# Grouped issue of the small fp32 products in a two-layer hybrid decoder step

## The chip, the cores and the metric

The kernel runs on one core of one Trainium2 chip. The metric is device microseconds of one execution; the time before is the median of 3 runs. The engines of the profile are PE (matrix products, with PEld its weight loads), DVE (vector), ACT (scalar and activations), POOL and SP; times are in us.

## The reference, cut to what matters

One inference step over a prompt of 512 tokens and 8 samples of 8 tokens each. A layer is

```
h    = rmsnorm(x); proj = h @ W_in             # 1024 -> all heads' inputs
mix  = [SSD(Mamba-2) | window attention | HGRN2 | RG-LRU](proj)
x    = x + mix @ W_out
x    = x + square(relu(rmsnorm(x) @ W_up)) @ W_down
```

and there are two of them, then a last RMSNorm. The change touches two of the four mixers:

```
# window attention: 4 blocks of 128 queries, a block sees its own and the previous 128 keys
logits = q k^T * 64**-0.5 + rel_bias(masked)   # 4 heads
p      = softmax([logits, sink])[..., :-1];  o = p @ v
# the 8 samples do the same against their cached 128 keys and their own 8
# SSD: chunks of the prompt and the samples each add a state
states = einsum('bcshn,bcsh,bcshp->bchpn', B, decay_s, x * dt)
S      = S * chunk_decay + states
```

New states, keys and values are outputs beside y.

## The kernel before, in words

All 576 tokens (512 of the prompt, 64 of the samples) lie as columns, and the features on partitions. Each large projection (`product`, L329 to L348) is done in three products of a high and a low part, 128x128 weights against 288 columns at a time, and this is most of what PE does: 8712 of its products are such "projection products" (tiles `pi` input, `pd` output and part of the down projection, `p` and `pu` MLP, `pl` the last), and 928 program-level matmuls are small fp32 products of the mixers. An fp32 product of the program shows as more than one record in the trace.

The kernel is written in a framework whose scheduler puts every engine's instructions into one fixed order when the program is built. It goes by the order in which the code issues them, except that `high_priority` lifts an instruction, and it lets an instruction overtake others whose inputs or buffers it holds to be later; `issue_after(x)` forbids those in its scope to stand ahead of x on x's engine. On the chip each engine then goes through its list strictly in order and waits at an instruction whose inputs are not there. So projection products fill the places on PE where a mixer's small product is not ready yet, as far as some are left that may run.

PSUM is split into 3 banks for projections (`mmbank`) and 5 for everything else (`bank`). The output projection (`outproj`, L1015) comes in two halves: `outproj(0)` needs only HGRN2 and SSD and has 192 products in a layer; `outproj(1)` needs RG-LRU and the attention and has 192 too, of which, by the three banks, 18 can run on the RG-LRU's part before the attention's output `mixh` exists. These 384 are what can fill PE while the attention (`swa`, L892 to L1012) works.

In `swa` the samples come first: 64 scores `ls`, the softmax in the tiles `L` (exponentials L941, scales L949), eight transposes `pts` (L954) copied to `PT`, values `aos`. Then four blocks of the prompt as generators, run by `staggered` (L138): scores `lg` (L978) and their masked maximum on DVE (L982); softmax (`ng` L985, exponentials L988 on ACT, `mx` L990, `sm` on DVE to L992); then a head at a time the scale on ACT (L1000), its transposes `pt` on PE (L1002), the copy to `PT` (L1003), at last the values `ao` (L354, from `tiled`) and the cast to `mixh` (L1008). The generators run one step apart, so that a block's scores, its neighbour's softmax and the next one's transposes are issued in turn. `PT` has 3 buffers and `L` has 4; a block takes two of each.

In the SSD, `dtt` (L685) is 15 small transposes of dt and its sums; `su` (L781) is a chunk's state and `sus` (L793) the samples'; `y` (L354) is the output's group of products.

Of the kernel before, what the change touches and what calls it, by code (L numbers as in the profile page):

```python
# [2 lines left out]

# [1 line left out]

# [8 lines left out]
AF = mybir.ActivationFunctionType  # L14
# [6 lines left out]
NP_ = 512  # L21
NB, NT = 8, 8
# [10 lines left out]
SLOT = 608  # L33
# [98 lines left out]
def seqs(t, w=NT):  # L132

    o = NP_ if w == NT else NP_ + 3
    return t[:, o : o + NB * w].rearrange("p (b t) -> p b t", b=NB)


def staggered(parts):  # L138

    n = 0  # L140
    while parts:
        n += 1
        for p in parts[:n]:
            if next(p, True):
                parts.remove(p)
                n -= 1


class Kern:
# [200 lines left out]
    def tiled(self, products):  # L350


        for n, (out, w, x) in enumerate(products):
            self.nc.tensor.matmul(out, w, x, start=n < 2, stop=n >= len(products) - 2, skip_group_check=True)  # L354

    def silu(self, out, in_):
        return self.nc.scalar.activation(out, in_, AF.Silu)
# [292 lines left out]
    def ssd_dt(self):  # L650

        nc, V, S, P = self.nc, self.nc.vector, self.nc.scalar, self.ssp
        dt, t1 = (P.t("b", SLOT, bufs=2)[:4, :T] for _ in range(2))
        ac, ed = (P.t("c", 640, bufs=SC)[:4, :T] for _ in range(2))
        rs = P.t("Bt", 640)[:4, :T]
        self.dma(rs, self.I["reset"])
        for h in range(2):
            a = slice(TH * h, TH * h + TH)
            ps = self.bank("pdt")[:4, :TH]
            nc.tensor.matmul(ps, self.con("sel4"), self.dtq[:, a], start=True, stop=True)  # L660
            V.tensor_tensor(dt[:, a], ps, self.rs[:4, a], op=ALU.mult)
        V.tensor_scalar(dt, dt, self.par("dtb", 0, 4), None, op0=ALU.add)
        S.activation(t1, dt, AF.Abs)
        S.activation(t1, t1, AF.Exp, scale=-1.0)
        S.activation(t1, t1, AF.Ln, bias=self.c1[:4])
        V.scalar_tensor_tensor(dt, dt, 0.0, t1, op0=ALU.max, op1=ALU.add)
        na = self.small([4, 1], "na")
        S.activation(na, self.par("alog", 0, 4), AF.Exp)
        V.tensor_scalar(na, na, -1.0, None, op0=ALU.mult)
        V.tensor_scalar(t1, dt, na, None, op0=ALU.mult)  # L670
        V.tensor_tensor_scan(ac, rs, t1, 0.0, op0=ALU.mult, op1=ALU.add)
        for a, w in ((slice(0, NP_), 128), (slice(NP_, T), NT)):
            cv = ac[:, a].rearrange("p (n t) -> p n t", t=w)
            V.tensor_tensor(ed[:, a].rearrange("p (n t) -> p n t", t=w),
                            cv[:, :, w - 1 : w].broadcast_to(list(cv.shape)), cv, op=ALU.subtract)
        S.activation(ed, ed, AF.Exp)
        dr = self.acd = self.dp.tile([4, T], F32, name=f"acd{self.li}")
        self.q(QC).dma_start(dr, ac)

        p2 = self.bank("dtt")  # L680
        pv = p2[:, :60].rearrange("p (c w h) -> p c w h", c=5, w=3)
        for ci in range(5):
            n = 128 if ci < 4 else NS
            for w, t in enumerate((dt, ac, ed)):
                nc.tensor.transpose(pv[:n, ci, w], t[:, 128 * ci : 128 * ci + n], self.ident[:4, :4])  # L685
        self.dtt = self.small([128, 5, 3, 4], "dtt")
        S.copy(self.dtt[:, :4], pv[:, :4])
        S.copy(self.dtt[:64, 4], pv[:64, 4])

        self.cs, self.el = [], self.small([128, 2, 12], "el")  # L690
        self.acj = self.small([128, 2, NS], "acj")
        for j in range(2):
            t = P.t("cs", T, bufs=2)
            for g in range(2):
                self.q(QC).dma_start(t[64 * g : 64 * g + 64], dr[2 * g + j].partition_broadcast(64))
                self.q(QC).dma_start(self.acj[64 * j : 64 * j + 64, g], dr[2 * g + j, NP_:T].partition_broadcast(64))
            S.activation(t, t, AF.Exp)
            V.tensor_copy(self.el[:, j, :4], t[:, :NP_].rearrange("p (c t) -> p c t", c=4)[:, :, 127])
            self.cs.append(t)
        S.activation(self.acj, self.acj, AF.Exp)  # L700

    def ssd(self):
        nc, V, S, li, P = self.nc, self.nc.vector, self.nc.scalar, self.li, self.ssp
# [22 lines left out]
        Bt = P.t("Bt", 640)  # L726
# [6 lines left out]
        for ci in range(4):  # L733
            a = slice(128 * ci, 128 * ci + 128)
            for g in range(2):
                nc.tensor.matmul(G[g][:, a], B[64 * g : 64 * g + 64, a], C[64 * g : 64 * g + 64, a], start=True, stop=True)
        for g in range(2):
            rg = slice(64 * g, 64 * g + 64)
# [36 lines left out]
            V.tensor_tensor(vs(xs[:64, NP_:640]), vs(p2[:64, :128]), ws(0), op=ALU.mult)  # L775
            V.tensor_tensor(vs(xd[:64, NP_:640]), vs(xs[:64, NP_:640]), ws(2), op=ALU.mult)

            for ci in range(4):
                a = slice(128 * ci, 128 * ci + 128)
                pu = self.bank("su")  # L780
                nc.tensor.matmul(pu[rg, :128], Bt[:, 128 * ci + 64 * g : 128 * ci + 64 * g + 64], xd[:, a], start=True, stop=True)  # L781
                if ci == 0:
                    V.tensor_copy(new[ci][rg], pu[rg, :128].rearrange("p (j n) -> p j n", j=2))
                    continue
                for j in range(2):
                    V.scalar_tensor_tensor(new[ci][rg, j], new[ci - 1][rg, j], self.el[rg, j, ci : ci + 1],
                                           pu[rg, 64 * j : 64 * j + 64], op0=ALU.mult, op1=ALU.add)
            S0 = P.t("S0", [NB, 64])
            self.dma(S0, self.I["sS0"][li, :, g])
            ve = P.t("b", SLOT, bufs=2)  # L790
            self.by_sequence(ve, Bt[:64, NP_ + 64 * g : NP_ + 64 * g + 64])
            ps = self.bank("sus")
            nc.tensor.matmul(ps, xd[:64, NP_:640], ve[:64, :512], start=True, stop=True)  # L793
            V.tensor_tensor(S0, S0, self.acj[:, g].rearrange("p (b t) -> p b t", b=NB)[:, :, NT - 1 : NT].broadcast_to([128, NB, 64]), op=ALU.mult)
            V.tensor_tensor(S0, S0, ps.rearrange("p (b n) -> p b n", b=NB), op=ALU.add)
            self.dma(self.O["sssm"][li, g], S0.rearrange("p b n -> p (b n)"))
# [95 lines left out]
    def swa(self, Q, K, Vv):  # L892
# [53 lines left out]
        for i in range(2):  # L946
            for u in range(2):
                l = Ls[i][:, u, :192]
                S.activation(l, l, AF.Copy, scale=sm[:, i, u : u + 1])  # L949
        pc, pn = P.t("PT", [2, 256], bufs=3), P.t("PT", [2, 256], bufs=3)  # L950
        for dst, rows, a in ((pc, 128, slice(0, 128)), (pn, 64, slice(128, 192))):
            ps = self.bank("pts")
            for k in range(4):
                nc.tensor.transpose(ps[:rows, 128 * k : 128 * k + 128], Ls[k // 2][:, k % 2, a], self.ident)  # L954
            S.copy(dst[:rows].rearrange("p a n -> p (a n)"), ps[:rows])
        p2 = self.bank("aos")
        kv = lambda i: slice(64 * i, 64 * i + 64)
# [8 lines left out]
        sk0 = PC["sink"][0]  # L966
        sinks = self.prm[:, li, sk0 : sk0 + 4]

        def block(nb):
            s0, n = (128 * (nb - 1), 256) if nb else (0, 128)  # L970
            nk = n // 128
            a = slice(128 * nb, 128 * nb + 128)
            L = [P.t("L", [2, 256], bufs=4) for _ in range(2)]
            mx, sm, ng = (self.small([128, 4], c) for c in ("mx", "sm", "ng"))
            lg = [self.bank("lg").rearrange("p (e n) -> p e n", e=2) for i in range(2)]
            for e in range(2):
                for i in range(2):
                    nc.tensor.matmul(lg[i][:, e, :n], Q[e][kv(i), a], K[kv(i), s0 : s0 + n], start=True, stop=True)  # L978
            for i in range(2):
                for e in range(2):  # L980
                    h = 2 * i + e
                    V.tensor_tensor_reduce(out=L[i][:, e, :n], in0=lg[i][:, e, :n], in1=bias[:, h, 256 - n :], scale=1.0,  # L982
                                           scalar=sinks[:, h : h + 1], op0=ALU.add, op1=ALU.max, accum_out=mx[:, h : h + 1])
            yield
            V.tensor_scalar(ng, mx, -1.0, None, op0=ALU.mult)  # L985
            for h in range(4):
                l = L[h // 2][:, h % 2, :n]
# [2 lines left out]
            S.activation(mx, mx, AF.Exp)  # L990
            V.tensor_tensor(sm, sm, mx, op=ALU.add)
            V.reciprocal(sm, sm)  # L992
            yield
            PT = [P.t("PT", [2, 256], bufs=3) for _ in range(2)]
            for i in range(2):
                pt = self.bank("pt").rearrange("p (e n) -> p e n", e=2)
                for e in range(2):
                    h = 2 * i + e
                    l = L[i][:, e, :n]
                    S.activation(l, l, AF.Copy, scale=sm[:, h : h + 1])  # L1000
                    for k in range(nk):
                        nc.tensor.transpose(pt[:, e, 128 * k : 128 * k + 128], l[:, 128 * k : 128 * k + 128], self.ident)  # L1002
                S.copy(PT[i][:, :, :n], pt[:, :, :n])  # L1003
            po = self.bank("ao").rearrange("p (e n) -> p e n", e=2)[:, :, :128]
            at = lambda i, k: s0 + 128 * k + 64 * i
            self.tiled([(po[kv(i), e], vt[:, at(i, k) : at(i, k) + 64], PT[i][:, e, 128 * k : 128 * k + 128])
                        for k in range(nk) for e in range(2) for i in range(2)])
            S.copy(oh[:, :, a], po)  # L1008
            V.tensor_tensor(ol[:, :, a], po, oh.bitcast(F32)[:, :, a], op=ALU.subtract)

        staggered([block(nb) for nb in range(4)])
        return oh, ol  # L1012


# [380 lines left out]
```

## Time and profile before

| | |
|---|---|
| median of 3 runs | 1359.47 us (1356.86 to 1362.58) |
| profiled execution | 1355.2 us, its span 1353.4 us |
| TensorE granted clock, mean | 0.998 of full |
| PE busy | 1328.0 us, 98% |
| DVE busy | 1028.5 us, 76% |
| ACT busy | 658.2 us, 49% |
| DMA, mean | 97 GB/s |

PE is busy in every fortieth of the span but the first, where it starts at 7 us. The other engines have room on the average. A row of a timeline gives start, duration, engine, line, operation, the tile written from the tiles read, the size, and in brackets the idle time ahead of it with what ended that; consecutive rows of one kind are merged with a count.

### The profile page before, as it was taken

The page shows a single profiled execution, that of the slowest core. Times are in us where ns is not written, and L with a number is a line of the kernel's source. Part 1 is how long each engine was busy: PE and PEld are TensorE (multiplying, and loading weights), DVE is VectorE, ACT ScalarE, POOL GpSimd, SP SyncE. Part 2 cuts the span into 40 slices and gives each one's busy share as a digit, 9 for nine tenths or more (in the row PEclk, how much of TensorE's full clock was granted, in tenths as well). Part 3 has the DMA queues.
Part 4 walks back from the last instruction along what each step waited for, and adds up shares of the span by engine and source line. Part 5 has one row for each costly group of instructions (what it writes and reads, how often), then busy time and mean ns, then how long its engine had stood idle before and what let it go on. Part 6 is the DMA issues. An engine that isn't in the chain of part 4 may idle for free.

```text
span 1353.4 us, 25452 instructions
## 1 busy us (share of the span) xinstructions
PE 1328.0 (98%) x10384; PEld 1279.6 (95%) x10384; DVE 1028.5 (76%) x2043; ACT 658.2 (49%) x1175; POOL 63.3 (5%) x126
## 2 busy tenths in 40 slices
PE   7999999999999999999999999999999999999997
PEld 7999899799999999999999998988999999999997
DVE  7788888488678677776669678886977677777755
ACT  6565436766243334333354774477653243334325
POOL 2201102000000000000000001100000000000000
PEclk9999999999999999999999999999999999999999
DMA  6324414123213222322331233231223213222312
GB/s 237 104 87 139 165 68 144 48 79 110 77 65 110 78 92 81 113 75 86 131 121 47 98 117 128 94 111 48 79 81 123 78 63 109 79 82 91 115 58 71
DMA packets 39831, 131.36 MB, mean 97 GB/s; under 512 B 6089, under 2 KB 8241, under 8 KB 39681
## 3 DMA queue, kind: packets, MB, share of 16 engines
q1 hardware_dynamic: 29312, 102.12, 21.9%
q0 software_dynamic: 6512, 22.64, 5.0%
q10 hardware_dynamic: 3888, 4.97, 1.2%
q8 instruction: 82, 1.34, 0.4%
q14 instruction: 37, 0.30, 0.1%
HBM read 120.32 MB, written 11.34 MB: 97 GB/s over the span
## 4 chain that ended last, share of the span: by engine, by line
PE 86%; DVE 7%; ACT 3%; issue 2%; DMA 0%; SPq 0%; DVEq 0%; ACTq 0%
PE pd L339 33%; PE p L1102 21%; PE pi L339 15%; PE pu L339 6%; PE pl L1255 2%; PE sc L554 2%; DVE lo L326 1%; DVE a L444 1%; PE ss L402 1%; PE ao L354 1%; ACT hi L326 1%; DVE A L562 1%; DVE qE L550 1%; PE y L354 1%; PE lg L978 1%
## 5 line engine op out<-in xcount | busy, mean ns | idle before, releaser
L326 ACT CAST hi<-raw 128x1024 fp32r<-128x1024 f32 x134 | 140.2, 1046 | 297.1 <-PE pd L339 144.6
L339 PE MATMUL pd<-fh,hi 128*128 128x288 f32 x960 | 284.1, 296 | 0.0
L339 PE MATMUL pd<-fl,hi 128*128 128x288 f32 x960 | 284.0, 296 | 0.0
L339 PE MATMUL pd<-fh,lo 128*128 128x288 f32 x960 | 282.8, 295 | 0.0
L339 PE MATMUL pi<-xh,hi 128*128 128x288 f32 x704 | 210.6, 300 | 7.6 <-ACT xh L377 7.1
L339 PE MATMUL pi<-xl,hi 128*128 128x288 f32 x704 | 210.4, 300 | 1.1 <-DVE xl L378 1.1
L339 PE MATMUL pi<-xh,lo 128*128 128x288 f32 x704 | 211.1, 300 | 0.0
L326 DVE TENSOR_TENSOR lo<-raw,hi 128x1024 fp32r<-128x1024 f32 x134 | 163.6, 1222 | 27.3 <-ACT hi L326 26.7
L1037 DVE TENSOR_TENSOR x<-x,pd 128x288 f32<-128x288 f32 x240 | 108.2, 451 | 97.9 <-PE pd L339 97.8
L339 PEld LDWEIGHTS pd<-fh,lo 128*128 128x128 f32 x960 | 180.9, 188 | 0.0
L339 PEld LDWEIGHTS pd<-fh,hi 128*128 128x128 f32 x960 | 180.4, 188 | 0.0
L339 PEld LDWEIGHTS pd<-fl,hi 128*128 128x128 f32 x960 | 180.4, 188 | 0.0
L339 PEld LDWEIGHTS pi<-xh,hi 128*128 128x128 f32 x704 | 133.0, 189 | 10.1 <-ACT xh L377 7.1
L339 PEld LDWEIGHTS pi<-xh,lo 128*128 128x128 f32 x704 | 132.9, 189 | 6.0 <-issue 5.2
L339 PEld LDWEIGHTS pi<-xl,hi 128*128 128x128 f32 x704 | 132.9, 189 | 3.6 <-DVE xl L378 1.7
L1102 PE MATMUL p<-Th,ul 128*128 128x288 f32 x312 | 92.2, 296 | 0.0
L1102 PE MATMUL p<-Tl,uh 128*128 128x288 f32 x312 | 92.1, 295 | 0.0
L1102 PE MATMUL p<-Th,uh 128*128 128x288 f32 x312 | 92.0, 295 | 0.0
L1102 PE MATMUL p<-xl,uh 128*128 128x288 f32 x312 | 91.9, 295 | 0.0
L1102 PE MATMUL p<-xh,ul 128*128 128x288 f32 x312 | 91.9, 295 | 0.0
L1102 PE MATMUL p<-xh,uh 128*128 128x288 f32 x312 | 91.7, 294 | 0.0
L1078 ACT CAST uh<-raw 128x1024 fp32r<-128x1024 f32 x52 | 54.5, 1048 | 66.8 <-PE p L1102 43.2
(489 smaller groups left out, 3003.2 us busy)
## 6 DMA issues: line engine op xcount, KB each, us to landing
raw<-in_wu SPq DMA_DIRECT2D x64, 512.0 KB, 3.3
raw<-in_wd SPq DMA_DIRECT2D x64, 512.0 KB, 4.2
raw<-in_wi SPq DMA_DIRECT2D x44, 512.0 KB, 3.3
raw<-in_wo SPq DMA_DIRECT2D x16, 512.0 KB, 3.2
x<-in_xT SPq DMA_DIRECT2D x8, 288.0 KB, 5.9
a<-acd ACTq DMA_DIRECT2D x4, 576.0 KB, 4.5
xl<-in_xT POOLq DMA_DIRECT2D x8, 288.0 KB, 4.3
xd<-x POOLq DMA_DIRECT2D x8, 288.0 KB, 2.4
```

Of the source, the lines that this page charges most:

```text
L326: self.split_ins = nc.scalar.copy(hi, raw).ins, nc.vector.tensor_tensor(lo, raw, hi.bitcast(F32), op=ALU.subtract).ins
L339: self.nc.tensor.matmul(out, w, x[:, a], start=n == 0, stop=n == last)
L354: self.nc.tensor.matmul(out, w, x, start=n < 2, stop=n >= len(products) - 2, skip_group_check=True)
L402: nc.tensor.matmul(ps[:, :TH], ones, s[:, TH * h : TH * h + TH], start=n == 0, stop=n == len(sqs) - 1)
L444: V.scalar_tensor_tensor(dst[:, :CW], src[:, k : k + CW], w(k), dst[:, :CW], op0=ALU.mult, op1=ALU.add)
L550: V.tensor_tensor(qE[r, d, : W // 2].rearrange("p (n h) -> p n h", h=h), qu[r], eu[r], op=ALU.mult)
L554: nc.tensor.matmul(pv[:, :, 64 * ci : 64 * ci + 64], kE[:, 128 * ci : 128 * ci + 128], qE[:, :, 64 * ci : 64 * ci + 64], start=True, stop= ...
L562: V.copy_predicated(Av[:, d], m, ps[:, d].rearrange("p (n h) -> p n h", h=h))
L1037: self.nc.vector.tensor_tensor(y[:, a], x[:, a], ps, op=ALU.add)
L1078: S.copy(hl[0], src)
L1102: nc.tensor.matmul(ps[:, :TH], u, x, start=j == 0, stop=j == 11)
L1255: nc.tensor.matmul(ps, u[:, o + q], v[:, a], start=j == 0, stop=j == 11)
```

## The change

A helper `together` issues the first of a list of products, and the others behind it on PE. With it
- the 15 transposes `dtt` are one group;
- the samples' state product `sus`, with its load of `S0` and `by_sequence`, is issued ahead of the four `su` of its group, and these stand behind it;
- the eight `pts` of the samples are one group over two banks, so that all four scales must have been done;
- a block's transposes `pt` are one group behind all four scales of the block; the values of the block ahead of it and the scores of the block two on stand behind the group's first transpose; `PT` has 4 buffers; `staggered` is gone, and the order is written out.

```diff
+    def together(self, calls):
+
+        first = calls[0]().ins
+        with self.tc.issue_after(first):
+            for c in calls[1:]:
+                c()
+        return first
...
+        calls = []
         for ci in range(5):
             n = 128 if ci < 4 else NS
             for w, t in enumerate((dt, ac, ed)):
-                nc.tensor.transpose(pv[:n, ci, w], t[:, 128 * ci : 128 * ci + n], self.ident[:4, :4])
+                calls.append(partial(nc.tensor.transpose, pv[:n, ci, w], t[:, 128 * ci : 128 * ci + n], self.ident[:4, :4]))
+        self.together(calls[::-1])
...
+            ps = self.bank("sus")
+            first = nc.tensor.matmul(ps, xd[:64, NP_:640], ve[:64, :512], start=True, stop=True).ins
             for ci in range(4):
                 a = slice(128 * ci, 128 * ci + 128)
                 pu = self.bank("su")
-                nc.tensor.matmul(pu[rg, :128], Bt[:, 128 * ci + 64 * g : 128 * ci + 64 * g + 64], xd[:, a], start=True, stop=True)
+                with self.tc.issue_after(first):
+                    nc.tensor.matmul(pu[rg, :128], Bt[:, 128 * ci + 64 * g : 128 * ci + 64 * g + 64], xd[:, a], start=True, stop=True)
...
-        pc, pn = P.t("PT", [2, 256], bufs=3), P.t("PT", [2, 256], bufs=3)
-        for dst, rows, a in ((pc, 128, slice(0, 128)), (pn, 64, slice(128, 192))):
-            ps = self.bank("pts")
-            for k in range(4):
-                nc.tensor.transpose(ps[:rows, 128 * k : 128 * k + 128], Ls[k // 2][:, k % 2, a], self.ident)
+        pc, pn = P.t("PT", [2, 256], bufs=4), P.t("PT", [2, 256], bufs=4)
+        parts = [(self.bank("pts"), *x) for x in ((pc, 128, slice(0, 128)), (pn, 64, slice(128, 192)))]
+        self.together([partial(nc.tensor.transpose, ps[:rows, 128 * k : 128 * k + 128], Ls[k // 2][:, k % 2, a], self.ident)
+                       for ps, dst, rows, a in parts for k in (3, 2, 1, 0)])
+        for ps, dst, rows, a in parts:
             S.copy(dst[:rows].rearrange("p a n -> p (a n)"), ps[:rows])
...
+        def turned(L, mx, s0, n, a):
+            PT = [P.t("PT", [2, 256], bufs=4) for _ in range(2)]
+            pt = [self.bank("pt").rearrange("p (e n) -> p e n", e=2) for i in range(2)]
+            first = self.together([partial(nc.tensor.transpose, pt[i][:, e, 128 * k : 128 * k + 128],
+                                           L[i][:, e, 128 * k : 128 * k + 128], self.ident)
+                                   for i in (1, 0) for e in (1, 0) for k in range(n // 128)])
+            for i in (1, 0):
+                S.copy(PT[i][:, :, :n], pt[i][:, :, :n])
+            return first, PT
...
+            with self.tc.issue_after(behind) if behind else nullcontext():
+                self.tiled([(po[kv(i), e], vt[:, at(i, k) : at(i, k) + 64], PT[i][:, e, 128 * k : 128 * k + 128])
+                            for k in range(n // 128) for e in range(2) for i in range(2)])
...
-        staggered([block(nb) for nb in range(4)])
+        blocks = [scores(0), scores(1)]
+        softmax(*blocks[0])
+        old = None
+        for nb in range(4):
+            first, PT = turned(*blocks[nb])
+            if old:
+                values(*old, first)
+            if nb < 3:
+                softmax(*blocks[nb + 1])
+            if nb < 2:
+                blocks.append(scores(nb + 2, first))
+            old = PT, *blocks[nb][2:]
+        values(*old)
```

`scores`, `softmax` and `values` hold the lines of the old `block`, except that the scales on ACT now end `softmax`.

On PE the attention's last block of layer 1 stood like this before, with projection products `pd` between a block's transposes `pt` (the numbers behind a name count its tiles):

```order
L339 MATMUL pd_1534_10857<-mixh_1383_9906,lo1532_10840 128x288
L339 MATMUL pd_1535_10871<-mixh_1383_9906,hi1532_10839 128x288
L339 MATMUL pd_1535_10871<-mixl_1384_9907,hi1532_10839 128x288
L339 MATMUL pd_1535_10871<-mixh_1383_9906,lo1532_10840 128x288
L339 MATMUL pd_1535_10871<-mixh_1383_9906,hi1532_10839 128x288
L339 MATMUL pd_1535_10871<-mixl_1384_9907,hi1532_10839 128x288
L1002 MATMUL pt_1483_10497<-cst_449,L_1462_10427 128x128 x2
L339 MATMUL pd_1535_10871<-mixh_1383_9906,lo1532_10840 128x288
L1002 MATMUL pt_1483_10497<-cst_449,L_1462_10427 128x128 x2
L1002 MATMUL pt_1484_10505<-cst_449,L_1463_10428 128x128 x4
L354 MATMUL ao_1485_10513<-PT_1481_10495,vt_1422_10239 64x128
```

On PE now, in layer 1, from the second block's transposes to the first of the third's:

```order
L348 MATMUL pt_1469_10440<-cst_449,L_1449_10372 128x128
L351 MATMUL pt_1469_10440<-cst_449,L_1449_10372 128x128 x3
L351 MATMUL pt_1468_10439<-cst_449,L_1448_10371 128x128 x4
L344 MATMUL ao_1470_10451<-PT_1455_10399,vt_1422_10239 64x128
L344 MATMUL ao_1470_10451<-PT_1456_10400,vt_1422_10239 64x128
L344 MATMUL ao_1470_10451<-PT_1455_10399,vt_1422_10239 64x128
L344 MATMUL ao_1470_10451<-PT_1456_10400,vt_1422_10239 64x128
L979 MATMUL lg_1476_10476<-x_1403_10049,x_1408_10108 128x256
L979 MATMUL lg_1477_10477<-x_1403_10049,x_1408_10108 128x256
L979 MATMUL lg_1476_10476<-x_1403_10049,x_1413_10167 128x256
L979 MATMUL lg_1477_10477<-x_1403_10049,x_1413_10167 128x256
L348 MATMUL pt_1481_10489<-cst_449,L_1462_10425 128x128
```

No `pd` stands between one block's group and the next one's any more; this holds in layer 1 from the first scores to the last values, and in layer 0 from the third block's transposes on.

On ACT in layer 1 the samples' softmax (tiles `L_1434`, `L_1435`, sums `sms`) stood ahead of the RG-LRU's last steps (`m`, and the cast to `mixh_1383` a few rows further on) before:

```order
L941 ACTIVATE L_1434_10267,sms_1432_10265<-L_1434_10267,ngs_1433_10266 128x192 x2
L941 ACTIVATE L_1435_10268,sms_1432_10265<-L_1435_10268,ngs_1433_10266 128x192 x2
L943 ACTIVATE mxs_1431_10264<-mxs_1431_10264 128x4
L872 ACTIVATE m_1388_9911<-m_1388_9911 128x2x600
L949 ACTIVATE L_1434_10267<-L_1434_10267,sms_1432_10265 128x192
L873 ACTIVATE m_1388_9911<-m_1388_9911 128x2x600
```

The same place on ACT now:

```order
L457 CAST mixh_1383_9906<-gt_1389_9912 128x576
L884 COPY misc1_7842<-xc_1385_9908 128x1
L885 COPY misc1_7842<-xc_1385_9908 128x8
L316 CAST hi1532_10839<-raw1531_10837 128x1024
L457 CAST mixh_1383_9906<-gt_1389_9912 128x576
L942 ACTIVATE L_1434_10267,sms_1432_10265<-L_1434_10267,ngs_1433_10266 128x192 x2
```

The samples' exponentials now come behind the RG-LRU's output, and PE has more `pd` ahead of the group `pts`: between the samples' scores and the first `pts` stood 79 before and stand 161 now.

## Rows read from the trace of the kernel before

**Rows 1.** the page: PE's busy time, share and instructions

```profile
PE 1328.0 (98%) x10384; PEld 1279.6 (95%) x10384; DVE 1028.5 (76%) x2043; ACT 658.2 (49%) x1175; POOL 63.3 (5%) x126
```

**Rows 2.** PE's waits: waiting, releaser, us, times, longest us

```profile
PE pts L954 <- ACT L L949: 1.6, 2, 1.3
PE pt L1002 <- ACT L L1000: 1.6, 2, 0.8
PE y L354 <- issue: 1.5, 1, 1.5
```

**Rows 3.** windows of the two attentions, L339 alone: us, PE (x), PEld (x), PEclk

```profile
896.60:934.30 37.70, 23.15 (x136) 19.12 (x136) 1.00 0.13 45
238.15:271.70 33.55, 19.50 (x106) 15.23 (x106) 1.00 0.13 47
```

**Rows 4.** PE, layer 1's attention, from the timeline

```profile
896.63 0.44 PE L954 MATMUL pts<-cst,L 128*128 128x128 f32 x2 [0.28 <-ACT L L949]
901.34 0.65 PE L354 MATMUL aos<-PT,vt 64*64 64x256 f32 x4
902.96 1.58 PE L978 MATMUL lg<-x,x 64*128 64x128 f32 x16
926.47 1.58 PE L354 MATMUL ao<-PT,vt 128*64 128x128 f32 x16 [0.22 <-ACT PT L1003]
```

**Rows 5.** PE, a lone group of transposes in layer 1's SSD

```profile
780.78 0.30 PE L339 MATMUL pi<-xl,hi 128*128 128x288 f32 x1
781.45 0.30 PE L339 MATMUL pi<-xh,hi 128*128 128x288 f32 x1
781.58 0.60 PE L765 MATMUL xt<-cst,X 128*128 128x128 f32 x4
782.04 0.38 PE L339 MATMUL pi<-xl,hi 128*128 128x288 f32 x1
```

**Rows 6.** DVE, layer 0, scores of the first two blocks

```profile
243.07 0.35 DVE L982 CUSTOM_DVE_ANT_0 L<-lg,bias,prm 128x128 f32<-128x128 f32 x1 [2.25 <-PE lg L978]
244.60 0.48 DVE L982 CUSTOM_DVE_ANT_0 L<-lg,bias,prm 128x256 f32<-128x256 f32 x1
246.23 0.09 DVE L982 DVE_READ_ACCUMULATOR2_ANT mx<- 128x1 f32 x1
```

**Rows 7.** ACT, layer 0, exponentials of a 128-wide and a 256-wide block

```profile
244.48 0.40 ACT L988 ACTIVATE L<-L,ng 128x128 f32<-128x128 f32 x1 [3.83 <-DVE ng L985]
246.04 1.04 ACT L326 CAST hi<-raw 128x1024 fp32r<-128x1024 f32 x1
255.38 0.51 ACT L988 ACTIVATE L<-L,ng 128x256 f32<-128x256 f32 x1
257.35 0.19 ACT L990 ACTIVATE mx<-mx 128x4 f32<-128x4 f32 x1
```

**Rows 8.** ACT, layer 1, scales and copies

```profile
912.24 1.26 ACT L1000 ACTIVATE L<-L,sm 128x128 f32<-128x128 f32 x4
...
925.83 1.07 ACT L1003 COPY PT<-pt 128x512 f32<-128x512 f32 x2
929.35 0.19 ACT L990 ACTIVATE mx<-mx 128x4 f32<-128x4 f32 x1
930.04 1.71 ACT L1000 ACTIVATE L<-L,sm 128x256 f32<-128x256 f32 x4 [0.50 <-DVE sm L992]
```

**Rows 9.** PE, products near the start of the execution

```profile
9.45 0.44 PE L339 MATMUL pi<-xh,lo 128*128 128x288 f32 x1
9.69 0.44 PE L339 MATMUL pi<-xh,hi 128*128 128x288 f32 x1
...
12.27 0.30 PE L339 MATMUL pi<-xh,lo 128*128 128x288 f32 x1
```

**Rows 10.** windows behind the last product: us, PE, PEld, DVE, ACT, POOL, PEclk

```profile
1346.00:1347.00 1.00, 0.00 (x0) 0.00 (x0) 0.38 (x2) 0.55 (x2) 0.00 (x0) 0.89 0.00 0
1347.00:1348.00 1.00, 0.00 (x0) 0.00 (x0) 1.00 (x4) 0.00 (x0) 0.00 (x0) 0.50 0.00 0
```

More of the change, by code (lines that the diff above doesn't have):

```diff
@@ L2 @@
 from contextlib import ExitStack, nullcontext
+from functools import partial
 import numpy as np
@@ L135, in seqs @@
     return t[:, o : o + NB * w].rearrange("p (b t) -> p b t", b=NB)
[L138 to L146, printed above, removed]
 class Kern:
@@ L776, in ssd @@
             V.tensor_tensor(vs(xd[:64, NP_:640]), vs(xs[:64, NP_:640]), ws(2), op=ALU.mult)
+            S0 = P.t("S0", [NB, 64])
+            self.dma(S0, self.I["sS0"][li, :, g])
+            ve = P.t("b", SLOT, bufs=2)
+            self.by_sequence(ve, Bt[:64, NP_ + 64 * g : NP_ + 64 * g + 64])
+            ps = self.bank("sus")
+            first = nc.tensor.matmul(ps, xd[:64, NP_:640], ve[:64, :512], start=True, stop=True).ins
             for ci in range(4):
@@ L787, in ssd @@
                                            pu[rg, 64 * j : 64 * j + 64], op0=ALU.mult, op1=ALU.add)
[L788 to L793, printed above, removed]
             V.tensor_tensor(S0, S0, self.acj[:, g].rearrange("p (b t) -> p b t", b=NB)[:, :, NT - 1 : NT].broadcast_to([128, NB, 64]), op=ALU.mult)
@@ L967, in swa, with scores @@
         sinks = self.prm[:, li, sk0 : sk0 + 4]
-        def block(nb):
+        def scores(nb, behind=None):
             s0, n = (128 * (nb - 1), 256) if nb else (0, 128)
-            nk = n // 128
             a = slice(128 * nb, 128 * nb + 128)
             L = [P.t("L", [2, 256], bufs=4) for _ in range(2)]
-            mx, sm, ng = (self.small([128, 4], c) for c in ("mx", "sm", "ng"))
+            mx = self.small([128, 4], "mx")
             lg = [self.bank("lg").rearrange("p (e n) -> p e n", e=2) for i in range(2)]
-            for e in range(2):
-                for i in range(2):
-                    nc.tensor.matmul(lg[i][:, e, :n], Q[e][kv(i), a], K[kv(i), s0 : s0 + n], start=True, stop=True)
+            with self.tc.issue_after(behind) if behind else nullcontext():
+                for e in range(2):
+                    for i in range(2):
+                        nc.tensor.matmul(lg[i][:, e, :n], Q[e][kv(i), a], K[kv(i), s0 : s0 + n], start=True, stop=True)
             for i in range(2):
@@ L983, in block, with softmax @@
                                            scalar=sinks[:, h : h + 1], op0=ALU.add, op1=ALU.max, accum_out=mx[:, h : h + 1])
-            yield
+            return L, mx, s0, n, a
+        def softmax(L, mx, s0, n, a):
+            sm, ng = (self.small([128, 4], c) for c in ("sm", "ng"))
             V.tensor_scalar(ng, mx, -1.0, None, op0=ALU.mult)
@@ L992, in block @@
             V.reciprocal(sm, sm)
[L993 to L1003, printed above, removed]
+            for h in range(4):
+                l = L[h // 2][:, h % 2, :n]
+                S.activation(l, l, AF.Copy, scale=sm[:, h : h + 1])
@@ L1004, in block, with values @@
+        def values(PT, s0, n, a, behind=None):
             po = self.bank("ao").rearrange("p (e n) -> p e n", e=2)[:, :, :128]
             at = lambda i, k: s0 + 128 * k + 64 * i
-            self.tiled([(po[kv(i), e], vt[:, at(i, k) : at(i, k) + 64], PT[i][:, e, 128 * k : 128 * k + 128])
-                        for k in range(nk) for e in range(2) for i in range(2)])
+            with self.tc.issue_after(behind) if behind else nullcontext():
+                self.tiled([(po[kv(i), e], vt[:, at(i, k) : at(i, k) + 64], PT[i][:, e, 128 * k : 128 * k + 128])
+                            for k in range(n // 128) for e in range(2) for i in range(2)])
```

## Prediction

> **What bounds the kernel now.** I read the page's busy times first, then PE's waits, then the timeline of the attention on PE, and last ACT's and DVE's rows there. PE is busy in 1328.0 of 1353.4 us [rows 1], and its largest waits for a mixer are two of 1.6 us in sum and one of 1.5 us [rows 2]. So the kernel is a row of PE products without gaps. Nothing is won by making ACT or DVE faster, and any time in which PE finds nothing to do is added to the end one for one. A change of order can win what hand-overs between large and small products cost, and can lose by taking the large products away from the places where they filled a wait.
>
> A projection product follows the last one after 0.134 us: 780.78 to 781.45 is five of them [rows 5]. A lone group of five transposes costs 781.58 to 782.04 and a bit: from the product ahead of it to the second one behind it PE spends 0.81 us, of which two steps of 0.134 are the products' own, so 0.54 us or 0.109 per transpose. Going over to small products and back cost nothing there.
>
> In the attention the price is another. From the first `pts` to the end of the last `ao`, layer 1 takes 37.70 us with 136 projection products in it, and layer 0 33.55 us with 106 [rows 3]. Taking 0.134 for each, small products, hand-overs and waits cost 19.5 us in layer 1 and 19.3 in layer 0. Issued whole, the small products are worth: 8 `pts` at 0.109, 0.87; `aos` 1.62 (901.34 to 902.96 [rows 4]); scores of blocks 0 and 1, 1.58; the scores of blocks 2 and 3, 1.3 each (as many records as the 16 in 1.58 between them, with twice the columns, so an estimate above half of it); transposes 4 + 3 x 8 at 0.109, 3.05; values 0.8 + 3 x 1.45 (a little under the 1.58 of 16, whose last end is modelled) = 5.1. That is 14.8 us. Waits in layer 1's stretch are 1.3 (0.28 for `pts` and 0.22 for `ao` in [rows 4], 0.8 for `pt` in [rows 2]). So 3.4 us of its 19.5 are hand-overs, some 0.15 us for each of the about 22 groups there. This is all that grouping can win in a layer's attention.
>
> **What the change takes away.** The order on PE in layer 1 now has no `pd` from the first scores on: the four blocks stand in one piece, and the 384 products of the output projection that could stand between them are spent otherwise, 208 ahead of the first `pts`, 2 behind it, 174 after the last `ao`. They are spent early because on ACT the samples' softmax now stands behind the RG-LRU's casts, so `pts` comes 82 products later than before (161 ahead of it where 79 were). In layer 0 there are 6, 42, 28 and 1 between the groups, and none from the third block on. The four scales of a block must now be done ahead of its first transpose, where one did before.
>
> So I walk through layer 1's chain with PE empty, time 0 at the first `pts`. `pts` ends at 0.9, its two copies at 1.7 (1.07 for two [rows 8], the first beside the second bank's transposes), `aos` 1.7 to 3.3, the scores of blocks 0 and 1 to 4.9. DVE reads block 0's from 4.1; its four take 1.2 (243.07 to 244.60 less two small steps) and block 1's four, 244.60 to 246.23, another 1.63 [rows 6], and `ng` of block 0 now stands behind both: 7.1. Four exponentials of 128 take 1.56 (244.48 to 246.04 [rows 7]): 8.7. From `mx` to the first scale are 0.69 (929.35 to 930.04), four scales of 128 take 1.26 [rows 8]: 10.65. PE has waited 5.8 us from 4.9 on. Transposes of block 0 and scores of block 2 end at 12.4. On ACT follow the rest of block 1's exponentials (1.97 for four of 256 [rows 7], one of them done ahead of the scales), two copies, `mx` and 0.69, at 13.25 the scales of 256 (1.71 [rows 8]): 14.95, a wait of 2.5. Transposes, values of block 0 and scores of block 3 end at 17.9. Block 2's exponentials run from 17.1 to 19.1, its scales to 21.7: a wait of 3.8. Transposes and values of block 1 end at 24.0; block 3's scales at 27.4: a wait of 3.4. Transposes and the values of blocks 2 and 3 end at 31.2. With 0.6 for the copies ahead of `aos` the waits are 16.1; 14.8 + 16.1 = 30.9 against 19.5: **layer 1 loses 11.4 us**.
>
> In layer 0 the waits ahead of the first two groups of transposes are filled by the 42 and 28 products (5.6 and 3.8 us against 5.8 and 2.5), those ahead of the third and the fourth, 3.8 + 3.4 = 7.2, are not. 14.8 + 7.2 = 22.0 against 19.3: **layer 0 loses 2.7 us**.
>
> Both ends for these two terms. The most that the chain can shrink is by ACT never waiting inside it: exponentials 7.5, scales 6.4, copies of blocks 0 to 2 2.8, four `mx` 0.6 make 17.3 from 7.1 on, so the last transposes come at 24.4 instead of 27.4, and 1.6 earlier again if block 0's `ng` did not cost block 1's four. That is -4.6 in each layer. The other end: ACT's casts of weights, 1.04 each [rows 7], fall between a block's steps once or twice in a layer, and `pts` finds the samples' scales late (below): +5 in all.
>
> **The rest.** The whole program goes from 122 groups of small products to 77 by the order; 37 of the 45 lie in the attention and are in the terms above, 8 in the SSD and its neighbourhood: `dtt`, `su` with `sus`. At 0 (the lone group) to 0.45 us each; I take the attention's 0.15: -1.2. `sus` and `su` now stand directly ahead of layer 0's `y` there, where PE once waited 1.5 us [rows 2]: this may go or come again, +-1.5, taken as 0. The fourth `PT` buffer and the copies in another order hide behind the chain. No DMA is added; `S0`'s load is issued some us earlier on a queue that the chain doesn't touch. ACT and DVE have the same instructions as before.
>
> Sum at full clock: 11.4 + 2.7 - 1.2 = +12.9 us.
>
> **The clock.** Near the start PE's products follow each other at 0.24 us, 9.45 to 9.69, and by 12.27 a record is 0.30 long instead of 0.44 [rows 9]; behind the last product, in a stretch where PE has nothing to do, the granted clock is 0.89 in 1346 to 1347 and 0.50 in the next microsecond [rows 10], that is 1.2 GHz. So with nothing to do the clock falls soon, and the waits of before were too short to show more. Waits of 5.8, 3.8 and 3.4 us with 2 to 3 us of small products between them may well do it. The cost: on the way back some twelve products (9.45 to 12.27) at 0.24 instead of 0.134, 1.3 us for a layer; and the chain's own small products at half speed, of which 3.05 us of transposes and the last 2.9 of values are on the path and the rest lies in waits, up to 5.4 in layer 1 and 4 in layer 0. Together 1.3 to 12; I take 5, near layer 1's 6.7 less what hides in waits.
>
> The Trainium skill ("TensorE: Matmul & The Clock Gate", section "HAM oscillation — how this bites in real kernels") says that waits between bursts of products drop the clock to half and that the price is paid at each burst anew; by it the sum has the 5 us, and without it nothing. It speaks against this change; that the fall at the end of the trace agrees with it is the one thing that before can show.
>
> **The forecast.** The profiled execution took 1355.2 us, and the sum is made against it: 1355.2 + 12.9 + 5 = 1373.1. The median of the runs lies 4.3 above that execution, so 1377.4 as the runs are timed; I write 1377.
>
> **The rivals.**
> A, the forecast: layer 1's attention stalls, layer 0's end does, and the clock falls in it: 1373 to 1386. For it: the order and ACT's durations. 0.57.
> B, the stalls without the clock: the bursts of small products between the waits keep it up. 1359.5 + 12.9 = 1372.4, between 1367 and 1376. For it: no wait up to 1.5 us lowered it in before; against it: the fall behind the last product. 0.26.
> C, not slower: the stalls are mostly not there, because ACT, which in layer 0 stood idle 3.83 us ahead of block 0's exponentials [rows 7], runs the chain without a wait, and `ng` goes ahead. Then layer 1 loses 11.4 - 4.6 = 6.8, layer 0 wins 1.9, the SSD 1.2 and the 1.5 of `y`: +2.2, 1361.7, within half a per cent. It decides if the last transposes of layer 1 come earlier than some 24 us after its first `pts`. Against it: every step of the chain hangs on the one ahead of it, and scores of the block two on are issued behind transposes. 0.09, and 0.05 for a gain by a way that I don't see.
> D, worse: the products ahead of layer 1's `pts` are done before the samples' scales are. These are now behind the RG-LRU's last cast; its softmax takes 3.5 to 4.4 us (exponentials, 0.69 and scales of a block [rows 7, 8]) and only the 18 products of the RG-LRU's part, 2.4 us, can lie beside it. +2 to +4 on A: 1379 to 1390. 0.03.
>
> **How the numbers follow.** A 0.57, B 0.26, C 0.09, a gain 0.05, D 0.03. A and most of B lie between 1367 and 1386. For 8 in 10 I go from 1363, which takes in B and a part of C, to 1388, with most of D; the likeliest one's own range is 1373 to 1386. A change of 0.5%, some 6.8 us, is about what a measurement of this kernel can tell from none: faster 0.05, same 0.10 (C and the edge of B), slower 0.85.
>
> **What would show it.** In the profile after, PE's waits should have `pt` for L's scales at 12 to 16 us over eight groups, layer 1's first near 5.8; the windows from first `pts` to last `ao` should give about 31 and 22 us outside projection products; the granted clock in the waits of layer 1 should go to 0.5 and the products behind the last `ao` stand 0.24 apart for A, and stay at 1.00 for B. It is wrong if PE's waits on `pt` stay under 5 us in sum, if projection products stand at 0.134 around every group, or if the time is lost outside the two attentions.

## The result, and the profile after

The changed kernel takes 1377.62 us (median of 5 runs, 1374.76 to 1378.87) against 1356.89 before (5 runs): a ratio of 1.0141, 95% interval 1.0118 to 1.0163. It is 20.7 us slower, and the forecast was 1377. The profiled execution took 1378.87 us, 23.7 over that of before.

The page of the kernel after, PE's busy time and its clock over 40 slices of the span:

```profile
PE 1330.4 (97%) x10384; PEld 1285.6 (93%) x10384; DVE 1028.7 (75%) x2043; ACT 660.1 (48%) x1175; POOL 63.1 (5%) x126
...
PEclk9999999899999999999999999996999999999999
```

PE is busy 2.4 us longer than in [rows 1] in a span 23.2 us longer, so in the sum nearly all of the loss shows as PE standing still (the busy time holds both what the groups save and what slower products add, and does not part them); the slices with clock 8 and 6 are the two attentions. PE's waits after, to set beside [rows 2]:

```profile
PE pt L348 <- ACT L L999: 20.9, 8, 5.8
PE pts L348 <- ACT L L950: 2.4, 2, 1.3
PE y L344 <- issue: 1.4, 1, 1.4
```

The waits for the scales ahead of `pt` went from 1.6 us in two to 20.9 in eight. Two windows, from the first `pts` of a layer to the first projection product behind the last `ao`, with the projection products' line alone (us, PE busy and count, PEld, granted clock, DMA share, GB/s), answer to [rows 3]:

```profile
918.13:954.35 36.22, 0.51 (x2) 0.30 (x3) 0.67 0.04 15
239.15:274.92 35.77, 11.26 (x78) 10.37 (x78) 0.81 0.11 36
```

Layer 1 has 2 projection products where it had 136. With 0.134 us taken off for each (77 start inside layer 0's window), small products, hand-overs and waits cost 36.0 us in layer 1 (19.5 before) and 25.5 in layer 0 (19.3): +16.5 and +6.1 before rounding. That is 22.6 of the 23.2 us, and 0.6 lie elsewhere. The timeline of PE in layer 1, after:

```profile
918.13 0.33 PE L348 MATMUL pts<-cst,L 128*128 128x128 f32 x1 [1.07 <-ACT L L950]
...
921.56 1.58 PE L979 MATMUL lg<-x,x 64*128 64x128 f32 x16
928.92 0.47 PE L348 MATMUL pt<-cst,L 128*128 128x128 f32 x1 [5.78 <-ACT L L999]
...
929.96 2.08 PE L979 MATMUL lg<-x,x 64*128 64x256 f32 x8
933.23 0.47 PE L348 MATMUL pt<-cst,L 128*128 128x128 f32 x1 [1.19 <-ACT L L999]
...
941.70 0.48 PE L348 MATMUL pt<-cst,L 128*128 128x128 f32 x1 [3.76 <-ACT L L999]
...
948.84 0.47 PE L348 MATMUL pt<-cst,L 128*128 128x128 f32 x1 [3.27 <-ACT L L999]
...
950.74 3.68 PE L344 MATMUL ao<-PT,vt 128*64 128x128 f32 x32
954.35 0.48 PE L329 MATMUL pd<-mixh,hi 128*128 128x288 f32 x1
954.67 0.29 PE L329 MATMUL pd<-mixl,hi 128*128 128x288 f32 x1
954.80 0.29 PE L329 MATMUL pd<-mixh,lo 128*128 128x288 f32 x1
```

The brackets are the four waits: 5.78, 1.19, 3.76 and 3.27 us, against 5.8, 2.5, 3.8 and 3.4 in the forecast. A group of eight transposes takes 1.9 us (948.84 to 950.74) where 0.87 was worked out. The clock is the reason; windows of a microsecond in the first wait (us, then PE, PEld, DVE, ACT, POOL, clock):

```profile
926.00:927.00 1.00, 0.00 (x0) 0.00 (x0) 0.00 (x0) 1.00 (x8) 0.00 (x0) 1.00 0.00 0
927.00:928.00 1.00, 0.00 (x0) 0.00 (x0) 0.34 (x2) 0.99 (x5) 0.00 (x0) 0.62 0.00 0
928.00:929.00 1.00, 0.08 (x1) 0.08 (x2) 0.00 (x0) 1.00 (x4) 0.00 (x0) 0.50 0.00 0
```

PE stands still from 923.14 on, and the granted clock goes from 1.00 to 0.50, that is from 2.4 to 1.2 GHz, four microseconds later. First DVE reads the scores (busy until 925.6), and from 925.4 on ACT is at work almost without a gap: the chain is these maxima and ACT's exponentials and scales.

### The profile page after: what moved, and what is told of

The parts are those of the page before. It is cut to its first block, busy times and chain, and to the rows that moved or that the text cites. A ratio compares the mean times of both kernels' runs of the same rounds, so it can differ in the third digit from the quotient of the medians.

```text
span 1376.6 us, 25442 instructions
## 1 busy us (share of the span) xinstructions
PE 1330.4 (97%) x10384; PEld 1285.6 (93%) x10384; DVE 1028.7 (75%) x2043; ACT 660.1 (48%) x1175; POOL 63.1 (5%) x126
## 4 chain that ended last, share of the span: by engine, by line
PE 87%; ACT 5%; DVE 5%; issue 2%; DMA 1%; ACTq 0%; DVEq 0%
PE pd L329 31%; PE p L1124 21%; PE pi L329 18%; PE pu L329 6%; PE sc L552 2%; PE pl L1277 2%; PE ao L344 1%; ACT L L999 1%; PE ss L400 1%; DVE lo L316 1%; ACT hi L316 1%; PE pt L351 1%; PE y L344 1%; DVE L L983 1%; DMA cs<-acd 1%
## 5 line engine op out<-in xcount | busy, mean ns | idle before, releaser
L316 DVE TENSOR_TENSOR lo<-raw,hi 128x1024 fp32r<-128x1024 f32 x134 | 163.6, 1222 | 29.7 <-ACT hi L316 29.1
L329 PEld LDWEIGHTS pi<-xl,hi 128*128 128x128 f32 x704 | 132.7, 189 | 2.3 <-DVE xl L376 1.6
```

The costliest lines, as they stand in the source:

```text
L316: self.split_ins = nc.scalar.copy(hi, raw).ins, nc.vector.tensor_tensor(lo, raw, hi.bitcast(F32), op=ALU.subtract).ins
L329: self.nc.tensor.matmul(out, w, x[:, a], start=n == 0, stop=n == last)
```

## The experiments

The theory is the prediction's: what decides is where projection products stand on PE, and the groups are not bad by themselves. Every ratio is against executions of the kernel before taken together with the run; their medians lie within 0.5 us of each other. "Small and idle" is the window of a layer's attention less 0.134 us for each projection product.

| run | median, us | ratio, 95% interval | small and idle, layer 0 / layer 1 |
|---|---|---|---|
| before | 1356.5 to 1357.0 | 1 | 19.3 / 19.5 |
| changed | 1377.62 | 1.0141 (1.0118 to 1.0163) | 25.5 / 36.0 |
| su_only | 1375.94 | 1.0130 (1.0108 to 1.0153) | 19.3 / 33.3 |
| attn_only | 1371.78 | 1.0104 (1.0086 to 1.0122) | 24.2 / 29.1 |
| dtt_only | 1357.10 | 0.9998 (0.9987 to 1.0010) | 19.3 / 19.5 |
| warm | 1368.38 | 1.0078 (1.0061 to 1.0094) | 21.2 / 29.1 |
| held_b | 1357.25 | 0.9999 (0.9990 to 1.0008) | 14.9 / 26.0 |
| samples_first | 1358.12 | 1.0011 (1.0001 to 1.0020) | 14.9 / 27.5 |
| softmax_first | 1349.53 | 0.9947 (0.9935 to 0.9960) | 15.3 / 16.0 |
| two_blocks_first | 1349.27 | 0.9944 (0.9930 to 0.9958) | 15.5 / 16.4 |
| before_softmax_first | 1353.36 | 0.9976 (0.9967 to 0.9986) | 17.3 / 18.3 |
| softmax_first_old_ssd | 1349.24 | 0.9947 (0.9935 to 0.9959) | 15.3 / 16.2 |

**The parts one at a time.** `su_only` is the kernel before with `sus` ahead of `su`, `dtt_only` that with dt's transposes grouped, `attn_only` the changed kernel without these two.

```diff
# su_only, on the kernel before
+            ps = self.bank("sus")
+            first = nc.tensor.matmul(ps, xd[:64, NP_:640], ve[:64, :512], start=True, stop=True).ins
             for ci in range(4):
...
+                with self.tc.issue_after(first):
+                    nc.tensor.matmul(pu[rg, :128], ...)
```

> The kernel before with one edit alone: the samples' state product ahead of the four chunk states. Theory (the time goes where the projection products leave the attention's waits, whatever moves them): by the order layer 1's attention has no projection product between the groups from the first scores to the third block's values, although its code is that of before, so layer 1 loses 7 to 11 us against the kernel before, with a clock that falls there, and layer 0 nothing: 1364 to 1369. Rival (an edit in the SSD touches the SSD alone and saves hand-overs): 1355 to 1358, PE's waits on pt as before.

> The attention's part of the change alone, dtt, su and sus as before. Theory: layer 0 as in the changed kernel (+6); in layer 1 82 projection products stand in the first wait, and the waits ahead of the third and fourth block stay empty, so it loses about what layer 0 loses: together +11 to +14 against before, 1368 to 1371. Rival (the attention's grouping is the whole loss, the SSD's part gives nothing or a gain): 1377 to 1379.

> The kernel before with the 15 transposes of dt as one group and nothing else; by the order both attentions stand as in before. Theory (a merged group is worth some 0.15 us): 1355 to 1358, no difference that can be measured. Rival (any edit of the order moves the attention's filling): 1362 or more.

`su_only` lost 19.0 us, more than either theory had. Its windows (columns as above):

```profile
916.85:955.25 38.40, 9.07 (x38) 7.00 (x38) 0.73 0.04 15
244.05:277.58 33.53, 19.47 (x106) 15.22 (x106) 1.00 0.14 47
```

Layer 0's attention is to a tenth what it was; layer 1's, in whose code nothing was changed, has 38 projection products for 136 and 33.3 us for 19.5. Ungrouped transposes on PE in layer 1, with their waits:

```profile
927.23 1.35 PE L1003 MATMUL pt<-cst,L 128*128 128x128 f32 x4 [3.69 <-ACT L L1001]
...
934.75 1.97 PE L1003 MATMUL pt<-cst,L 128*128 128x128 f32 x8 [2.19 <-ACT L L1001]
```

So an edit in the SSD moved the filling of a stage that comes more than 100 us later (layer 1's first `sus` is at 800.5). ACT shows by which step: with the SSD's edit alone the samples' exponentials (`ngs`) stand behind the RG-LRU's last cast to `mixh`, as in the changed kernel, and with the attention's edit alone they stand ahead of the RG-LRU's last steps (`m`), as in before. First `su_only`, then `attn_only`:

```profile
913.30 0.68 ACT L459 CAST mixh<-gt 128x576 fp32r<-128x576 f32 x1 [2.01 <-DVE gt L888]
913.88 0.45 ACT L942 ACTIVATE L<-L,ngs 128x192 f32<-128x192 f32 x1
```

```profile
899.33 0.46 ACT L939 ACTIVATE L<-L,ngs 128x192 f32<-128x192 f32 x1
902.37 1.21 ACT L870 ACTIVATE m<-m 128x1200 f32<-128x1200 f32 x1 [1.07 <-DVE sms L942]
```

Between the samples' scores and `pts` stand 146 projection products in `su_only` and 103 in `attn_only`, for 79 in before and 161 in the changed kernel. Why the scheduler moves the softmax for an edit in the SSD is not shown. The 7 to 11 us expected were too little: layer 1 lost 13.8, with the chain at half clock, whose price in this run was not measured apart. In this profile the clock is also at half for 3.4 and 6.8 us in layer 0's SSD (129.3 to 132.7 and 156.7 to 163.5), where time less 0.134 us for each projection product, from the first `dtt` to `kts`, a product at the attention's start, is 49.6 us for 44.7 in before. `attn_only` lost 14.8, a little over the 11 to 14 expected, and not as expected: layer 1 lost twice what layer 0 did (29.1 - 19.5 and 24.2 - 19.3), where the same had been named for both. The two losses add up to 33.8, more than the 20.7 of the whole change. In the windows layer 1 loses 13.8 and 9.6 apart and 16.5 together, since they empty in part the same waits, and the clock does not fall in layer 0's SSD of the changed kernel. `dtt_only` changes nothing in the median, as expected. But three of its 11 executions had a granted clock of 0.998 and took 1354.5 to 1355.6 us, and eight had 0.993 to 0.996 and took 1355.9 to 1360.7; in its profile, one of the eight, the clock is at half for 6.8 us in layer 0's SSD (154 to 162).

**The clock by itself.** `warm` fills most of the waits with products that do nothing.

```diff
+                for _ in range(WARM[li][nb]):    # [[0, 0, 11, 13], [24, 8, 15, 13]]
+                    dummy = nc.tensor.matmul(pt[0][:, 0, :128], self.ident, self.ident, start=True, stop=True).ins
+            with self.tc.issue_after(dummy):
                 first = self.together([...])
```

> The changed kernel with products of the identity matrix, overwritten afterwards, put into PE's empty waits ahead of the transposes: 11 and 13 ahead of layer 0's third and fourth block, 24, 8, 15 and 13 in layer 1. They are shorter than the waits and need nothing that comes late. Theory (some 8.5 us of the loss is the clock at 1.2 GHz in the small products of the chain): the granted clock is 1.00 in both attentions, the two stretches shrink from 36.2 and 35.8 to about 31 and 32.5, and the time is 7 to 9 us under the changed kernel's, 1368 to 1371. Rival (the chain is ACT's and DVE's, and PE's clock is hidden in waits): within 2 us of the changed kernel, though the clock is full.

```profile
914.63:944.00 29.37, 0.51 (x2) 0.30 (x2) 1.00 0.06 19
240.01:271.55 31.54, 11.24 (x78) 10.38 (x78) 1.00 0.13 42
```

```profile
919.58 5.62 PE L1009 MATMUL pt<-cst 128*128 128x128 f32 x48
925.43 0.33 PE L350 MATMUL pt<-cst,L 128*128 128x128 f32 x1 [0.23 <-ACT L L1001]
...
941.14 0.27 PE L350 MATMUL pt<-cst,L 128*128 128x128 f32 x1
...
942.11 1.97 PE L345 MATMUL ao<-PT,vt 128*64 128x128 f32 x32
944.00 0.40 PE L330 MATMUL pd<-mixh,hi 128*128 128x288 f32 x1
```

The clock is 1.00 in both windows, eight transposes take 0.97 us (941.14 to 942.11) instead of 1.90, the last two blocks' values 1.9 instead of 3.6, and the time falls by 9.2 us to 1368.38. It came out as expected; the rival, a clock hidden in waits, is out. The useful work and the chain are the same, so 9 of the 20.7 us are the clock, and the other 11.4 are the waits and what they displace.

**Filling the waits.** `samples_first` and `held_b` keep all groups of the change. `samples_first` puts the samples' softmax at high priority; `held_b` holds back half of `outproj(0)` besides.

```diff
+        with self.tc.high_priority(HP):
             for e in range(2):
                 S.copy(qs[:, :NB, e], seqs(Q[e]))
...
# held_b, besides: marks[0] is the first pts, marks[1] the first block's first pt; HELD = [None, None, 0, 1]
+            with self.tc.issue_after(self.marks[mark]) if mark is not None else nullcontext():
                 self.down(m2, wh, wl, xs, src, dst)
```

> The changed kernel with one edit: the samples' softmax at high priority. By the order layer 0's waits then hold 38, 23, 25 and 41 projection products, layer 1's 125, 3, 0 and 0. Theory (what fills the waits decides): layer 0's attention as in the run with held products, 4 to 5 us better than before; layer 1 waits some 1, 3.8 and 3.4 us ahead of the last three blocks with a clock that falls there, 8 us worse than before: 1358 to 1363 in all. Rival (the early samples are worth nothing by themselves): 1370 or more.

> The changed kernel with two edits: the samples' softmax at high priority, so that ACT and DVE do it ahead of the RG-LRU's last steps, and the last two quarters of the output projection's first half issued behind the first sample transpose and the first block's first transpose. By the order the waits ahead of the transposes then hold 38, 23, 25 and 41 projection products in layer 0 and 62, 1, 26 and 37 in layer 1. Theory (the groups save hand-overs of some 3 us a layer, and the whole loss was the missing filling): 1350 to 1359, the clock full, PE's waits on pt under 4 us in sum. Rival (waiting for four scales and issuing in groups is itself the loss): 1365 or more with waits on pt above 8 us.

One edit of the order takes back 19.5 of the 20.7 us. In both runs layer 0 needs 14.9 us for what took 19.3 before. Layer 1 of `samples_first` is 8.0 us worse than before, as expected: only its first wait is filled, and ahead of the last two blocks PE waits 3.75 and 3.27 us. PE's waits of `samples_first`:

```profile
PE pt L348 <- ACT L L1000: 9.9, 6, 3.8
PE pts L348 <- ACT L L951: 1.0, 2, 0.7
```

`held_b` came out in the range expected, but not as expected: the clock was not full (0.993), and PE waited 8.7 us for `pt`, where under 4 had been named. PE in layer 1 of `held_b`, the scores and the first transpose behind them, with 62 projection products between:

```profile
892.70 1.58 PE L981 MATMUL lg<-x,x 64*128 64x128 f32 x16
909.82 0.47 PE L349 MATMUL pt<-cst,L 128*128 128x128 f32 x1 [7.10 <-ACT L L1001]
```

and DVE at that time:

```profile
893.45 0.35 DVE L985 CUSTOM_DVE_ANT_0 L<-lg,bias,prm 128x128 f32<-128x128 f32 x1
...
893.73 2.71 DVE L883 TENSOR_TENSOR_SCAN xc<-r,i 128x600 f32<-128x600 f32 x2
...
901.75 0.34 DVE L985 CUSTOM_DVE_ANT_0 L<-lg,bias,prm 128x128 f32<-128x128 f32 x1
...
904.91 0.08 DVE L985 DVE_READ_ACCUMULATOR2_ANT mx<- 128x1 f32 x1
906.05 0.23 DVE L991 TENSOR_SCALAR ng<-mx 128x4 f32<-128x4 f32 x2
```

Block 0's first maximum runs at 893.45, then the RG-LRU's work from its two scans on goes ahead of the other three (901.75), and block 1's maxima and a weight's low part ahead of `ng` (906.05). PE waits 7.10 us in spite of 62 products, and the clock falls. So the remaining fault was on DVE, and the last runs put the maxima and each block's softmax at high priority too, in `two_blocks_first` for the first two blocks alone; nothing is held back in them.

```diff
# softmax_first, besides samples_first; before_softmax_first does the same in the kernel before
+            with self.tc.high_priority(HP):
                 for i in range(2):
                     for e in range(2):
...
                         V.tensor_tensor_reduce(...)
...
+            with self.tc.high_priority(HP):
                 V.tensor_scalar(ng, mx, -1.0, None, op0=ALU.mult)
...
```

> The changed kernel with the samples' softmax and each block's softmax (the maxima on DVE, exponentials and scales on ACT) at high priority; no product is held back. By the order the waits hold 42, 5, 26 and 24 projection products in layer 0 and 49, 8, 28 and 17 in layer 1. Theory (the one long wait left in the run with held products was layer 1's first, 7.1 us, behind RG-LRU's scans and a weight's low part on DVE, and the clock that fell with it): waits on pt under 4 us in sum, clock 0.998, both attentions 3 to 5 us shorter than before, 1346 to 1352. Rival (what the softmax overtakes on DVE and ACT, weights' parts and evictions, is then late for PE): 1355 to 1360 with new waits on hi, lo or the mm banks.

> As the run with every softmax first, but only the samples and the first two blocks of the prompt have the priority. By the order the waits hold 42, 5, 33 and 24, and 49, 8, 45 and 26. Theory: the same within 2 us, as the first two blocks decide where the projection products go. Rival (the last two blocks' softmax is late without it): 3 us or more slower than with all four, with waits ahead of the third and fourth.

> The kernel before, ungrouped and staggered, with the same priorities for the samples' and the blocks' softmax. Theory (the gain is in the groups, since hand-overs cost some 0.15 us each, and the priority only makes room for them): 1353 to 1357, with no more than layer 0's wait of 1.3 us for the samples gone. Rival (the priority is the whole gain and the groups are worth nothing): within 2 us of the grouped kernel with all softmax first.

> The grouped attention with every softmax first, but dtt, su and sus as in the kernel before. It prices the SSD's part of the change where the attention is filled. Theory (the SSD's groups are worth about what the stretch ahead of layer 1's attention shows, 0.8 us a layer, less 1 us that the products stand behind each other in layer 0): 1349 to 1352, 0 to 2 us over the kernel with all groups. Rival (the SSD's part costs time, as it did alone): 1340 to 1347.

`softmax_first` takes 1349.53 us, 7.2 less than before and 28.1 less than the changed kernel: the version that beats both. Its windows and waits:

```profile
890.02:922.28 32.26, 17.61 (x121) 16.25 (x122) 1.00 0.16 54
232.65:262.32 29.67, 15.75 (x107) 14.41 (x108) 1.00 0.17 58
```

```profile
PE pt L348 <- ACT L L1002: 2.6, 4, 1.5
PE pts L348 <- ACT L L951: 1.0, 2, 0.7
```

and those of the ungrouped kernel with the same priorities:

```profile
891.72:927.82 36.10, 21.63 (x134) 18.48 (x134) 1.00 0.18 58
230.61:266.76 36.15, 22.94 (x141) 19.58 (x141) 1.00 0.18 57
```

```profile
PE pts L955 <- ACT L L950: 1.1, 2, 0.7
PE pt L1006 <- ACT L L1004: 1.3, 2, 0.7
```

Both run at full clock with little waiting, so what is between them is the grouping: 15.3 and 16.0 us of small work against 17.3 and 18.3, and 1349.53 against 1353.36 in all. Of the 7.2 us, 3.4 come with the priority alone and 3.8 more with the groups on top of it. The expectation had left the priority 1.3 us and the rest to the groups; the priority alone takes 2.1 us off layer 0 and 1.2 off layer 1. `two_blocks_first` and `softmax_first_old_ssd` are the same within a microsecond: the first two blocks decide, and no gain or loss by the SSD's part of the change can be measured once the attention is filled.

## Why the prediction was right

The time, the sign and the likeliest case A are as forecast; point by point:

- **Layer 1's waits.** Right. Three of the four waits agree to 0.15 us; the second was 1.19 for 2.5 because the scores ahead of it ran at half clock (929.96 to 932.04). In `warm`, at full clock, it is 2.9 from the scores' end to the transposes. The forecast's waits were worked out for full clock; there, in `warm`, the four places are 5.8, 2.9, 3.4 and 2.9 us long, 15.0 for 15.5 in sum, so that the last two agree so closely at half clock is in part luck. The windows named as a sign, 31 and 22 us, came as 36.0 and 25.5, since they too were worked out at full clock. Layer 1 at full clock costs 29.1, where 30.9 was worked out: +9.6 instead of +11.4.
- **Layer 0.** Right: 21.2 at full clock for 22.0, +1.9 instead of +2.7. The 12 to 16 us of waits on `pt` named as a sign were too few: 20.9 came, 14.0 of them in layer 1 and 6.9 in layer 0. The working itself had 15.5 and 7.2; the sign left out layer 0's.
- **What grouping can win.** 3.4 us a layer were named as the most. The runs show 1.9 and 2.2 between the kernels with softmax first, and the grouped ones come to 15.3 and 16.0, near the 14.8 added up from single rows. In `samples_first` and `held_b` layer 0 wins 4.4 against before, waits taken in (before had one of 0.8 us ahead of `pt`).
- **The rest of the program.** -1.2 was said; the spans leave +0.6 outside the two windows, and the runs with and without the SSD's groups differ by 0.3 us. So this term was wrong in its sign, and small. What was not foreseen is that the SSD's edit alone empties layer 1's attention. The prediction named the right step, the samples' softmax behind the RG-LRU's casts, but read both orders as one change; in `su_only` this step comes from the SSD's edit, and in `attn_only` it is absent. The order of each part apart would have shown it. The step is also not the whole cause: with the samples first, layer 1's last two waits stay.
- **The clock.** It fell, as A said and B denied; the term was mis-sized, 5 us for 9.2, and its working was partly wrong. The twelve products at 0.24 us on the way back don't exist: behind the last values, projection products stand 0.13 apart from the second on (954.67 to 954.80); by then PE had worked without a gap since 948.84. So the price lies in the small products of the chain, which I had let the waits hide in part. The page "TensorE: Matmul & The Clock Gate" of the Trainium skill ("HAM oscillation — how this bites in real kernels") tells of bursts of products that each start at the low clock after a wait. The trace agrees: the group behind layer 1's first wait starts at 0.50, and `warm` prices the low clock at 9.2 us.
- **The basis.** The median of before was taken 4.3 us above its profiled execution, from three runs. Later medians of 1356.5 to 1357.0 put it 1.3 to 1.8 above. So the sum was short by about 2.8 us (17.9 for the measured 20.7; at full clock it was 1.5 too high, 12.9 for 11.4, and the clock 4.2 too low) and the basis high by 2.6. That 1377 is this near is luck: these errors cancel.
- **The rivals.** C asked for layer 1's last transposes 24 us after the first `pts`; they came 30.7 after. D asked for `pts` to wait 2 to 4 us more; it waited 1.07 for 0.28.

## What to carry to other kernels

Where one engine is always busy because large products fill the waits of small ones, a new order is judged by what stands in those waits afterwards: count the filling between the groups, and walk the chain with the durations of the other engines. Grouping small products does save their hand-overs (about 2 us for each attention here), but only if the chain that feeds the groups is put first on the engines that run it. A wait of a few microseconds costs more than itself when the clock falls in it (9 us beside 11 here), and an edit in one stage can move the filling of another, so each part of a change is compared in its order by itself.

## What the runs showed of the hardware

The clock does not follow PE's waiting closely. In the changed kernel it is back at 1.00 while PE has nothing to do, after 4.7 us of small products (933.23 to 937.94):

```profile
938.00:939.00 1.00, 0.00 (x0) 0.00 (x0) 1.00 (x5) 0.74 (x5) 0.00 (x0) 1.00 0.00 0
939.00:940.00 1.00, 0.00 (x0) 0.00 (x0) 0.97 (x8) 0.06 (x1) 0.00 (x0) 1.00 0.00 0
```

and in `softmax_first` it goes down in layer 0's SSD with PE at work, behind a wait of only 0.55 us and a group of transposes of four rows (PE's timeline, then a window in which the clock is at half):

```profile
116.22 0.19 PE L348 MATMUL dtt<-cst,c 4*64 4x4 f32 x1 [0.55 <-ACT c L674]
...
117.08 1.26 PE L248 MATMUL rb<-x,rb 32*128 32x128 f32 x8
118.27 1.11 PE L465 MATMUL tr<-cst,X 128*128 128x128 f32 x4
```

```profile
118.00:121.40 3.40, 3.40 (x23) 2.70 (x22) 0.88 (x4) 0.00 (x0) 2.44 (x6) 0.50 0.46 166
```

The four `tr` there take 1.11 us. In `two_blocks_first` the same group stands behind a wait of 0.56 us, the four `tr` take 0.66, and the clock is 1.00 from 118.0 to 121.4; in `attn_only`, where `dtt` is not grouped, it is at half from 112 to 115 with PE at work. So neither that wait nor the group decides by itself, and what does is open.
